# A dense PEER stage: one of four token blocks sums its down projection in two PSUM banks over all 128 chunks, the other blocks' sums take turns in four

## The chip, the cores and the metric

The kernel runs on one core of a Trainium2 chip. The metric is device time in microseconds, from the first to the last instruction with what lies around them. TensorE (PE) multiplies, VectorE (DVE) and ScalarE (ACT) do elementwise work, GpSimd (POOL) here mostly issues gathers, SyncE (SP) issues loads. PE writes only to PSUM, which has 8 banks of 128 partitions x 512 float32; DVE and ACT read it from there.

## What is computed

One decoder layer on 1024 tokens of 1024 floats: a token mixer (attention and a recurrence), and then PEER, a retrieval over 16,384 experts of one neuron each. The change touches only the last part:

```python
def blk(args):
    x_b, idx_b, g_b = args            # 128 tokens, 128 expert indices each, gates
    u = u_tab[idx_b]
    h = jax.nn.gelu(jnp.einsum('td,ted->te', x_b, u), approximate=False) * g_b
    return jnp.einsum('te,ted->td', h, v_tab[idx_b])
...
ffn = _peer_ffn(x, peer_w_q[l], peer_sub_keys[l], peer_u[l], peer_v[l])
x = _layer_norm(DEEPNORM_ALPHA * x + ffn, ln_ffn_g[l], ln_ffn_b[l])
```

`u_tab` and `v_tab` are 16,384 x 1024 float32.

## The kernel before

The eight blocks of 128 tokens are treated in two ways. Blocks 0, 1, 6 and 7 (`GATHER`) fetch the chosen rows of both tables by indirect DMA: per block 128 gathers of u rows (`gather_u`, L1105 on POOL), each reduced against the tokens by one DVE instruction (L1124), and then 128 gathers of v rows, each added into `ys` by one DVE instruction (L1149; the first by L1147, and `finish`, L1228, ends the block; block 0 does this on PE into the PSUM tile `y` instead). Eight tiles `rows` hold the rows under way.

Blocks 2 to 5 (`DENSE`, 512 tokens) compute all 16,384 experts as dense matmuls, with a matrix of gates that is zero where an expert was not chosen. The experts go in 128 chunks of 128, four chunks to a group (`JG`), 32 groups (`NG`). For each chunk, `up` loads 128 rows of u, splits them into a high and a low part (`uh` on ACT at L1031, `ul` on DVE at L1032), multiplies them with the tokens into a bank `psh` (8 slices, three matmuls each in `mm3`: L293, L294, L295), takes gelu (ACT, L1045), multiplies with the gates (DVE, L1047, `hs`), and splits again (`hh` on ACT, L1048, `hl` on DVE, L1049). `down` then works on a group in two halves `n` of 512 columns. For each chunk it loads and splits half the rows of v (`vh`, `vl`), and adds three matmuls for each of the four token blocks into that block's bank. After the four chunks of a half, DVE adds the four banks into `dy` in SBUF (L1064), which starts as the scaled residual. `finish_dense` normalises `dy` and writes it out.

PSUM's eight banks are pools: two `psh`, three `psf`, one `psv` (`BANKS`), and two for the tile `y` of `gather_v`. A half of `down` takes three `psf` and the `psv`.

The loop over groups takes two steps of `down` of the group before (a step is one chunk of one half), one chunk of `up`, and then `tick("dense")`, which lets the gathers of u and v rows of the other blocks emit 5.4 rows each a tick, while there are jobs. A scheduler then sets the order of each engine's instructions by its own estimates, so the order on an engine is fixed ahead of the run, and every engine works it off in order. The instructions on gathered rows keep their program order among each other.

Of the kernel before, what the change touches and what calls it, by code (L numbers as in the profile page):

```python
# [8 lines left out]
F32 = mybir.dt.float32  # L9
# [9 lines left out]
D = 1024  # L19
S = 1024  # L20
P = 128
# [45 lines left out]
ND = len(DENSE)  # L67
TD = ND * P
GS = float(2 ** 14)
JG = 4  # L70


class Layer:
# [249 lines left out]
    def mixers(self, groups, es):  # L323
# [6 lines left out]
        for n, (t0, T) in enumerate(groups):  # L330
# [48 lines left out]
            if T == 256:  # L379
                tail = self.tail_gather(t0, T, tail)  # L380
                if late:
                    return dense, tail, tl
                self.drain([tail])
                self.hold = HOLD
            else:
                self.tailed = False
                self.bjobs.append(self.tail_gbuild(tail, tl, gb))
# [631 lines left out]
    def dense(self, prep, tail, tl):  # L1019
        y, xh, xl = prep  # L1020
        nc, a = self.nc, self.a
        NG = P // JG
        dws = ExitStack()
        with self.pool("dw", 2, "left") as dw, dws:
            dv = {}
            def split(dw, src, n, name, bufs, raws):
                hi = dw.tile([P, n], F32R, name=name + "h", tag=name + "h", bufs=bufs)
                lo = dw.tile([P, n], F32R, name=name + "l", tag=name + "l", bufs=bufs)
                raw = dw.tile([P, n], F32, name=name + "r", tag=name + "r", bufs=raws)
                nc.sync.dma_start(raw, src)  # L1030
                nc.scalar.activation(hi, raw, AF.Copy)  # L1031
                nc.vector.tensor_tensor(lo, raw, hi.bitcast(F32), op=ALU.subtract)  # L1032
                return hi, lo

            def up(g):
                gt = dw.tile([P, TD // 32, JG, 32], F32, name="gt", tag="gt")
                nc.sync.dma_start(gt, self.d_g[:, :, g * JG : (g + 1) * JG, :].rearrange("q j i t -> j q i t"))
                for c in range(JG):
                    hh, hl = (dw.tile([P, TD], F32R, name=n, tag=n, bufs=JG + 2) for n in ("hh", "hl"))
                    uh, ul = (t.rearrange("p (c j) -> p c j", c=DC) for t in split(dw, a["ut"][g * JG + c], D, "u", 2, 3))  # L1040
                    ps = self.bank("h")[:, :TD]
                    for dc in range(DC):
                        self.mm3(ps, uh[:, dc], ul[:, dc], xh[:, dc], xl[:, dc], dc == 0, dc == DC - 1)
                    hs = dw.tile([P, TD], F32, name="hs", tag="hs")
                    nc.scalar.activation(hs, ps, AF.Gelu)  # L1045
                    h3 = hs.rearrange("p (q t) -> p q t", t=32)
                    nc.vector.tensor_tensor(h3, h3, gt[:, :, c], op=ALU.mult)  # L1047
                    nc.scalar.activation(hh, hs, AF.Copy)  # L1048
                    nc.vector.tensor_tensor(hl, hs, hh.bitcast(F32), op=ALU.subtract)  # L1049
                    yield hh, hl  # L1050

            def down(g, hs):
                for n in range(2):
                    ns = slice(n * 512, (n + 1) * 512)
                    acc = [self.bank("f") for _ in range(ND - 1)] + [self.bank("v")]
                    for c in range(JG):
                        r0 = (g * JG + c) * P
                        vh, vl = split(dv[0], a["v"][r0 : r0 + P, ns], 512, "v", 2, VRAW)
                        for tb in range(ND):
                            ts = slice(tb * P, (tb + 1) * P)  # L1060
                            self.mm3(acc[tb], hs[c][0][:, ts], hs[c][1][:, ts], vh, vl, c == 0, c == JG - 1)
                        yield
                    for tb in range(ND):
                        nc.vector.tensor_tensor(y[:, tb, ns], y[:, tb, ns], acc[tb], op=ALU.add)  # L1064
                        if g == NG - 1:
                            self.ln_stats(dv[1], tb, y[:, tb], (n,))

            def late():
                yield from tail
                tl.close()  # L1070
                dv[0] = dws.enter_context(self.pool("dv", 2, "left"))
                self.lnf = self.ffn_rows([dv[0].tile([P, D], F32, name=n, tag=n, bufs=1) for n in ("dlg", "dlb")])

            late, c0 = late(), 0
            prev = iter(())
            for g in range(NG + 1):
                cur = up(g) if g < NG else iter(())
                live, h = True, []
                while live:
                    live = False  # L1080
                    for _ in range(2):
                        if next(prev, self) is not self:
                            live = True
                    r = next(cur, self)
                    if r is not self:
                        live = True
                        h.append(r)
                    if live:
                        self.tick("dense", None, W0 if g == 0 else 1.0)
                    if c0 != 2:  # L1090
                        next(late, None)
                    c0 += 1
                self.drain([late])
                if g == NG - 1:
                    dv[1] = dv[0].tile([P, ND, 2, 6], F32, name="lnst", tag="lnst", bufs=1)
                if h:
                    prev = down(g, h)
            self.finish_dense(dv[0], y, dv[1])
# [218 lines left out]
```

## Time and profile before

| | |
|---|---|
| Median of 3 runs | 3072.04 us (3071.37 to 3078.85) |
| The profiled execution | 3059.49 us, of which 3057.6 from the first to the last instruction |
| Busy: PE, DVE, ACT, POOL | 85%, 87%, 36%, 53% |
| Mean granted TensorE clock | 0.921 of full |
| HBM traffic | 289 GB/s over the span |

"Busy" is the share of the span in which an engine ran something. PE's matmuls are pipelined, and one's end overlaps the next one's start, so for PE the distance from start to start says more than busy time. The same holds, less so, for DVE.

### The profile page before, as it was taken

To read this page: it belongs to the slowest core of one execution; us is meant where nothing else is said; L and a number is where in the kernel's file an instruction comes from. 1 tells how busy PE (TensorE), PEld (TensorE's weight loads), DVE (VectorE), ACT (ScalarE), POOL (GpSimd) and SP (SyncE) were. 2 spreads that over 40 slices of the span, in tenths; PEclk is the share of its full clock that TensorE was granted. 3 is DMA by queue.
4 is the path that set the end of the run, shared out by engine and by line. 5 is a ranking of instruction groups with operands and counts; after the bars stand their busy time and mean duration, and the time that the engine had idled before them with its cause. 6 is when DMAs were issued, how large, how long until landed. Compare 5 with 4: busy or idle time off the path is not lost.

```text
span 3057.6 us, 45196 instructions
## 1 busy us (share of the span) xinstructions
PE 2614.2 (85%) x15865; PEld 2140.4 (70%) x15865; DVE 2667.8 (87%) x5555; ACT 1091.4 (36%) x2068; POOL 1612.5 (53%) x1216
## 2 busy tenths in 40 slices
PE   7778699877669768779578999899989999999995
PEld 6768589755567545568457878777768877877874
DVE  8658776588778998689898999899999999999998
ACT  4733222365312233677522323232223323223321
POOL 2344377655665645110156666565476665656652
PEclk9878899878889879889789999999999999999998
DMA  7632499855877867865589999999999999999994
GB/s 278 195 138 90 178 333 326 256 157 163 303 279 270 288 199 255 312 258 194 192 305 343 361 366 381 333 370 368 345 355 363 372 386 362 359 361 342 371 334 164
DMA packets 338660, 887.11 MB, mean 290 GB/s; under 512 B 29912, under 2 KB 124136, under 8 KB 336000
## 3 DMA queue, kind: packets, MB, share of 16 engines
q0 software_dynamic: 147456, 536.94, 48.3%
q1 hardware_dynamic: 185200, 338.38, 31.7%
q10 hardware_dynamic: 5776, 8.90, 0.8%
q8 instruction: 125, 2.05, 0.3%
q14 instruction: 103, 0.84, 0.1%
HBM read 821.67 MB, written 62.42 MB: 289 GB/s over the span
## 4 chain that ended last, share of the span: by engine, by line
PE 40%; DVE 37%; issue 9%; DMA 6%; ACT 4%; POOL 3%; SPq 0%; DVEq 0%; POOLq 0%; ACTq 0%
DVE ys L1149 7%; PE psf L294 6%; PE psf L295 6%; PE psf L293 5%; DVE rows L1124 5%; PE psh L293 5%; PE psh L295 5%; PE psh L294 5%; POOL rows L1105 2%; DMA rows<-in_u,gsel 1%; DVE tw L808 1%; DVE dy L1064 1%; PE psv L294 1%; PE psv L718 1%; PE psv L295 1%
## 5 line engine op out<-in xcount | busy, mean ns | idle before, releaser
L1105 POOL DMA_INDIRECT rows<-in_u,gsel x512 | 688.4, 1345 | 585.6 <-DVE rows L1124 368.8
L1105 POOL DMA_INDIRECT rows<-in_v,gsel x512 | 640.9, 1252 | 437.7 <-DVE ys L1149 271.2
L1124 DVE SCALAR_TENSOR_TENSOR rows<-rows,gx 128x1024 f32<-128x1024 f32 x512 | 635.6, 1291 | 36.6 <-DMA rows<-in_u,gsel 27.8
L1149 DVE SCALAR_TENSOR_TENSOR ys<-rows,sd,ys 128x1024 f32<-128x1024 f32 x381 | 491.2, 1289 | 0.6
L293 PE MATMUL psh<-dxh,uh 128*128 128x512 f32 x1024 | 403.0, 394 | 29.4 <-ACT uh L1031 16.6
L295 PE MATMUL psh<-dxh,ul 128*128 128x512 f32 x1024 | 401.1, 392 | 9.5 <-DVE ul L1032 9.4
L294 PE MATMUL psh<-dxl,uh 128*128 128x512 f32 x1024 | 400.6, 391 | 0.0
L294 PE MATMUL psf<-vl,hh 128*128 128x512 f32 x768 | 311.0, 405 | 42.2 <-DVE vl L1032 41.4
L1031 ACT ACTIVATE vh<-vr 128x512 fp32r<-128x512 f32 x256 | 161.8, 632 | 436.1 <-PE psv L295 396.1
L295 PE MATMUL psf<-vh,hl 128*128 128x512 f32 x768 | 306.4, 399 | 0.0
L293 PE MATMUL psf<-vh,hh 128*128 128x512 f32 x768 | 278.5, 395 | 10.7 <-DVE dy L1064 8.8
L1031 ACT ACTIVATE uh<-ur 128x1024 fp32r<-128x1024 f32 x128 | 135.8, 1062 | 405.1 <-PE psh L294 400.0
L293 PEld LDWEIGHTS psh<-dxh,uh 128*128 128x128 f32 x1024 | 193.6, 189 | 77.2 <-ACT hs L1045 20.4
L295 PEld LDWEIGHTS psh<-dxh,ul 128*128 128x128 f32 x1024 | 193.5, 189 | 50.4 <-DVE ul L1032 10.5
L294 PEld LDWEIGHTS psh<-dxl,uh 128*128 128x128 f32 x1024 | 193.5, 189 | 39.5
L294 PEld LDWEIGHTS psf<-vl,hh 128*128 128x128 f32 x768 | 148.1, 193 | 89.7 <-DVE vl L1032 59.0
L215 ACT ACTIVATE whi<-wraw 128x1024 fp32r<-128x1024 f32 x106 | 111.6, 1056 | 230.9 <-PE psf L294 64.8
L1032 DVE TENSOR_TENSOR vl<-vr,vh 128x512 fp32r<-128x512 f32 x256 | 170.7, 689 | 12.0 <-ACT vh L1031 11.9
L293 PEld LDWEIGHTS psf<-vh,hh 128*128 128x128 f32 x768 | 145.5, 190 | 48.1 <-DVE dy L1064 9.8
L218 DVE TENSOR_TENSOR wlo<-wraw,whi 128x1024 fp32r<-128x1024 f32 x60 | 81.8, 1365 | 100.8 <-ACT whi L215 98.0
L295 PEld LDWEIGHTS psf<-vh,hl 128*128 128x128 f32 x768 | 148.1, 193 | 29.8
L1032 DVE TENSOR_TENSOR ul<-ur,uh 128x1024 fp32r<-128x1024 f32 x128 | 156.6, 1224 | 11.5 <-ACT uh L1031 10.5
(342 smaller groups left out, 6156.5 us busy)
## 6 DMA issues: line engine op xcount, KB each, us to landing
ur<-in_ut SPq DMA_DIRECT2D x128, 512.0 KB
vr<-in_v SPq DMA_DIRECT2D x256, 256.0 KB
d_g<-slab SPq DMA_DIRECT2D x16, 2048.0 KB
gt<-d_g SPq DMA_DIRECT2D x32, 1024.0 KB
wraw<-in_wq SPq DMA_DIRECT2D x48, 512.0 KB
wraw<-in_wt SPq DMA_DIRECT2D x34, 512.0 KB
wraw<-in_wn SPq DMA_DIRECT2D x24, 512.0 KB
wraw<-in_wo SPq DMA_DIRECT2D x24, 512.0 KB
```

Source lines behind the costliest of these rows:

```text
L215: nc.scalar.activation(hi, raw, AF.Copy)
L218: eng.tensor_tensor(lo, raw, hi.bitcast(F32), op=ALU.subtract)
L293: mm(out, lh, rh, start=start, stop=False, **kw)
L294: mm(out, lh, rl, start=False, stop=False, **kw)
L295: mm(out, ll, rh, start=False, stop=stop, **kw)
L718: nc.tensor.matmul(pv[:, qb], ps[:, qb * P : (qb + 1) * P], V[:, kb], start=kb == 0, stop=kb == b0 + qb, skip_group_check=True)
L808: nc.vector.match_replace(w, out_v[:, 0:8], vals, FMIN)
L1031: nc.scalar.activation(hi, raw, AF.Copy)
L1032: nc.vector.tensor_tensor(lo, raw, hi.bitcast(F32), op=ALU.subtract)
L1105: self.nc.gpsimd.indirect_dma_start(out=t, out_offset=None, in_=tab, in_offset=bass.IndirectOffsetOnAxis(ap=idx, axis=0))
L1124: self.pin(nc.vector.scalar_tensor_tensor(u, u, 1.0, x2, op0=ALU.mult, op1=ALU.mult, accum_out=sd[:, n : n + 1]), "u")
L1149: self.pin(nc.vector.scalar_tensor_tensor(ys, v, h, ys, op0=ALU.mult, op1=ALU.add), "w")
```

## The change

Block 0 of the dense blocks (`tb == 0`) gets the two-bank PSUM tile `y`, one bank for each half, and keeps adding into it from the first chunk to the last: its first matmul of all starts the sum, its last ends it. Its banks are added into `dy` only in the last group. The other three blocks still start anew in every group and half, and are added to `dy` each time. Their six sums in a group take `psf`, `psf`, `psf` in the first half and `psv`, `psf`, `psf` in the second.

```diff
--- before.py
+++ after.py
@@ -1049,18 +1049,24 @@
                     nc.vector.tensor_tensor(hl, hs, hh.bitcast(F32), op=ALU.subtract)
                     yield hh, hl
 
+            whole = [None]
+
             def down(g, hs):
+                if g == 0:
+                    whole[0] = self.psy.tile([P, D], F32, name="y", tag="y")
                 for n in range(2):
                     ns = slice(n * 512, (n + 1) * 512)
-                    acc = [self.bank("f") for _ in range(ND - 1)] + [self.bank("v")]
+                    acc = [whole[0][:, ns]] + [self.bank("v" if n and tb == 1 else "f") for tb in range(1, ND)]
                     for c in range(JG):
                         r0 = (g * JG + c) * P
                         vh, vl = split(dv[0], a["v"][r0 : r0 + P, ns], 512, "v", 2, VRAW)
                         for tb in range(ND):
                             ts = slice(tb * P, (tb + 1) * P)
-                            self.mm3(acc[tb], hs[c][0][:, ts], hs[c][1][:, ts], vh, vl, c == 0, c == JG - 1)
+                            first, last = (g == 0, g == NG - 1) if tb == 0 else (True, True)
+                            self.mm3(acc[tb], hs[c][0][:, ts], hs[c][1][:, ts], vh, vl, first and c == 0,
+                                     last and c == JG - 1, skip_group_check=tb == 0)
                         yield
-                    for tb in range(ND):
+                    for tb in range(0 if g == NG - 1 else 1, ND):
                         nc.vector.tensor_tensor(y[:, tb, ns], y[:, tb, ns], acc[tb], op=ALU.add)
                         if g == NG - 1:
                             self.ln_stats(dv[1], tb, y[:, tb], (n,))
```

After the change lines behind `down` have numbers 6 higher (the adds are L1070, v rows L1155).

The order of instructions moves in the dense stage alone. On DVE, beside v rows, the end of a half, before: the four adds into `dy` (L1064) alternate with v rows (L1149).

```order
L1149 SCALAR_TENSOR_TENSOR ys<-rows,sd,ys 128x1024
L1064 TENSOR_TENSOR dy<-dy,psf 128x512
L1149 SCALAR_TENSOR_TENSOR ys<-rows,sd,ys 128x1024
L1064 TENSOR_TENSOR dy<-dy,psf 128x512
L1149 SCALAR_TENSOR_TENSOR ys<-rows,sd,ys 128x1024
L1064 TENSOR_TENSOR dy<-dy,psf 128x512
L1149 SCALAR_TENSOR_TENSOR ys<-rows,sd,ys 128x1024
L1064 TENSOR_TENSOR dy<-dy,psv 128x512
L1047 TENSOR_TENSOR hs<-hs,gt 128x512
```

The end of a half at a like place after the change (L1070 are the adds, L1155 the v rows):

```order
L1155 SCALAR_TENSOR_TENSOR ys<-rows,sd,ys 128x1024
L1070 TENSOR_TENSOR dy<-dy,psf 128x512
L1155 SCALAR_TENSOR_TENSOR ys<-rows,sd,ys 128x1024
L1070 TENSOR_TENSOR dy<-dy,psf 128x512
L1155 SCALAR_TENSOR_TENSOR ys<-rows,sd,ys 128x1024
L1070 TENSOR_TENSOR dy<-dy,psf 128x512
L1155 SCALAR_TENSOR_TENSOR ys<-rows,sd,ys 128x1024
L1047 TENSOR_TENSOR hs<-hs,gt 128x512
```

Three adds stand there instead of four; the v rows are as many.

On PE, the start of the second half of group 13, before: the up pass (`psh`) ends, then come the first matmuls of the half (L293, `vh`), one for each block, with two matmuls of the next chunk's up pass among them, and then the first that need `vl` (L294).

```order
L295 MATMUL psh<-dxh,ul 128x512
L293 MATMUL psf<-vh,hh 128x512 x3
L293 MATMUL psh<-dxh,uh 128x512
L294 MATMUL psh<-dxl,uh 128x512
L293 MATMUL psv<-vh,hh 128x512
L294 MATMUL psf<-vl,hh 128x512
L295 MATMUL psf<-vh,hl 128x512
```

The same place after the change, where `y` is block 0's bank:

```order
L295 MATMUL psh<-dxh,ul 128x512
L293 MATMUL y<-vh,hh 128x512
L294 MATMUL y<-vl,hh 128x512
L295 MATMUL y<-vh,hl 128x512
L293 MATMUL psv<-vh,hh 128x512
L294 MATMUL psv<-vl,hh 128x512
L295 MATMUL psv<-vh,hl 128x512
L293 MATMUL psf<-vh,hh 128x512
```

Each block's three matmuls now stand together, block 0's first, and nothing of the up pass stands among them; the first use of `vl` comes one matmul after the first use of `vh` instead of six.

## Rows read from the trace of the kernel before

**Rows 1.** The page: the span, busy time of each engine, and the busy tenths of PE and DVE in 40 equal slices of the span.

```profile
span 3057.6 us, 45196 instructions
...
PE 2614.2 (85%) x15865; PEld 2140.4 (70%) x15865; DVE 2667.8 (87%) x5555; ACT 1091.4 (36%) x2068; POOL 1612.5 (53%) x1216
...
PE   7778699877669768779578999899989999999995
...
DVE  8658776588778998689898999899999999999998
```

**Rows 2.** Busy time by stretch: us from the span's start, length, busy us (and instructions) of PE, PE's weight loads, DVE, ACT and POOL, the granted clock, the share of the DMA engines, and GB/s. Two stretches beside gathered u rows, three beside v rows, and the dense stage as a whole.

```profile
1830.00:1918.00 88.00, 87.83 (x386) 71.67 (x385) 81.70 (x133) 27.24 (x41) 56.97 (x42) 1.00 1.00 370
2305.00:2438.00 133.00, 132.64 (x579) 107.81 (x579) 130.45 (x213) 41.22 (x61) 90.71 (x65) 1.00 1.00 370
1980.00:2207.00 227.00, 220.47 (x960) 179.00 (x959) 224.54 (x248) 67.66 (x101) 132.79 (x106) 1.00 0.97 359
2535.00:2718.00 183.00, 177.15 (x771) 143.82 (x770) 180.93 (x200) 55.18 (x81) 107.05 (x88) 1.00 0.99 362
2769.00:2905.00 136.00, 132.69 (x579) 108.51 (x580) 134.73 (x151) 41.25 (x61) 91.92 (x66) 1.00 0.97 357
1560.00:3037.00 1477.00, 1405.47 (x6022) 1136.02 (x6020) 1427.36 (x1924) 428.40 (x632) 910.45 (x679) 0.98 0.96 353
```

**Rows 3.** Groups of instructions between 1560 and 3037 us: line, engine, operation, out<-in, shapes, count, then busy us and mean ns of one, then idle us before them and what ended most of it.

```profile
L1149 DVE SCALAR_TENSOR_TENSOR ys<-rows,sd,ys 128x1024 f32<-128x1024 f32 x381 | 491.2, 1289 | 0.6
...
L1032 DVE TENSOR_TENSOR vl<-vr,vh 128x512 fp32r<-128x512 f32 x256 | 170.7, 689 | 12.0 <-ACT vh L1031 11.9
...
L1032 DVE TENSOR_TENSOR ul<-ur,uh 128x1024 fp32r<-128x1024 f32 x122 | 149.4, 1225 | 4.4 <-ACT uh L1031 3.4
...
L1064 DVE TENSOR_TENSOR dy<-dy,psf 128x512 f32<-128x512 f32 x192 | 126.4, 681 | 1.6 <-PE psf L295 1.6
...
L1047 DVE TENSOR_TENSOR hs<-hs,gt 128x512 f32<-128x512 f32 x124 | 85.6, 691 | 2.1 <-ACT hs L1045 1.3
...
L1064 DVE TENSOR_TENSOR dy<-dy,psv 128x512 f32<-128x512 f32 x63 | 43.0, 682 | 0.0
```

**Rows 4.** Instructions of PE in order of time within an up pass: start us, us. Nineteen matmuls lie between these two.

```profile
2507.16 0.39 PE L293 MATMUL psh<-dxh,uh 128*128 128x512 f32 x1
...
2511.70 0.39 PE L295 MATMUL psh<-dxh,ul 128*128 128x512 f32 x1
```

**Rows 5.** Instructions of DVE in order of time, beside u rows (L1124) and then beside v rows (L1149): start us, us.

```profile
1904.71 1.22 DVE L1124 SCALAR_TENSOR_TENSOR rows<-rows,gx 128x1024 f32<-128x1024 f32 x1
...
1905.85 1.22 DVE L1124 SCALAR_TENSOR_TENSOR rows<-rows,gx 128x1024 f32<-128x1024 f32 x1
...
1907.00 1.88 DVE L1064 TENSOR_TENSOR dy<-dy,psf 128x512 f32<-128x512 f32 x3
...
2492.37 0.69 DVE L1064 TENSOR_TENSOR dy<-dy,psv 128x512 f32<-128x512 f32 x1
2492.97 1.28 DVE L1149 SCALAR_TENSOR_TENSOR ys<-rows,sd,ys 128x1024 f32<-128x1024 f32 x1
2494.16 0.69 DVE L1032 TENSOR_TENSOR vl<-vr,vh 128x512 fp32r<-128x512 f32 x1
2494.76 1.28 DVE L1149 SCALAR_TENSOR_TENSOR ys<-rows,sd,ys 128x1024 f32<-128x1024 f32 x1
...
2505.13 1.22 DVE L1032 TENSOR_TENSOR ul<-ur,uh 128x1024 fp32r<-128x1024 f32 x1
2506.26 1.28 DVE L1149 SCALAR_TENSOR_TENSOR ys<-rows,sd,ys 128x1024 f32<-128x1024 f32 x1
2507.46 0.68 DVE L1064 TENSOR_TENSOR dy<-dy,psf 128x512 f32<-128x512 f32 x1
```

**Rows 6.** Who waited for whom between 1560 and 3037 us: us in total, times, the longest.

```profile
POOL rows L1105 <- DVE ys L1149: 284.3, 287, 11.5
...
PE psf L294 <- DVE vl L1032: 41.4, 25, 7.6
...
PE psf L293 <- DVE dy L1064: 8.8, 5, 3.1
...
DVE ys L1147 <- DMA rows<-in_v,gsel: 6.8, 1, 6.8
...
PE psv L293 <- DVE dy L1064: 5.4, 3, 2.7
```

**Rows 7.** The switch between u and v rows: where the v blocks begin (L1147) and end (L1228) with the first and last start, and then DVE's and PE's instructions at the first switch, with the idle time before them and what ended it.

```profile
L1147 DVE TENSOR_SCALAR ys<-rows,sd x3: 743/744/755, 1919.2 to 2748.0; 128x1024 f32<-128x1024 f32 x3
...
L1228 DVE SCALAR_TENSOR_TENSOR rows<-rows,ys x3: 1217/1220/1220, 2204.8 to 3020.1; 128x1024 f32<-128x1024 f32 x3
...
1919.22 0.76 DVE L1147 TENSOR_SCALAR ys<-rows,sd 128x1024 f32<-128x1024 f32 x1 [6.80 <-DMA rows<-in_v,gsel]
...
1928.11 0.79 PE L294 MATMUL psf<-vl,hh 128*128 128x512 f32 x1 [6.33 <-DVE vl L1032]
```

**Rows 8.** Busy time in one piece of 10 us, columns as in Rows 2.

```profile
1990.00:2000.00 10.00, 10.00 (x45) 8.27 (x45) 9.96 (x12) 3.33 (x5) 8.48 (x6) 1.00 1.04 408
```

**Rows 9.** The last instructions of block 0's gather that read the PSUM tile `y` (ACT): count, ns min/median/max, first and last start.

```profile
L1199 ACT ACTIVATE rows<-y x12: 371/374/378, 1308.2 to 1313.6; 32x256 f32<-32x256 f32 x12
```

## The prediction, made before the changed kernel was run

> **What bounds the kernel now.** I read the page first. In its 40 slices both PE and DVE stand at 8 and 9 from the 22nd to the last but one [rows 1]: that is the dense stage, about 1550 to 3037 us, the only stage the change touches. Two engines that are both nearly full are told apart only inside a stretch, so I cut the stage into stretches that hold nothing but groups of four chunks, and counted PE's matmuls in each [rows 2]. A group has 192 matmuls: 4 chunks x 8 slices x 3 in the up pass, and 2 halves x 4 chunks x 4 blocks x 3 in the down pass. So a group lasts 192 x 88 / 386 = 43.8 us and 192 x 133 / 579 = 44.1 us in the two stretches where the gather beside it is of u rows, and 45.4, 45.6 and 45.1 us in the three where it is of v rows (the v blocks begin at L1147 and end at L1228 [rows 7]).
>
> Next, what each engine needs for one group. PE: 21 matmuls start within 4.54 us, 0.227 us apart [rows 4], so 192 take 43.6 us. DVE: its instructions overlap a little, so I take distances between starts, not durations [rows 5]: 0.60 us for each of the 512-wide ones (vl, hs, hl and the adds into dy), 1.13 for ul, 1.195 for a v row, 1.145 for a u row (1904.71 to 1907.00 is two). A group has 8 vl, 4 ul, 4 hs, 4 hl and 8 adds: 4.8 + 4.5 + 4.8 + 4.8 = 18.9 us. Gathered rows per group I counted in the order of DVE's instructions: the three v blocks (384 rows) stand beside 24, 23 and 22 chunks, 17.25 groups, so 22.3 rows or 26.6 us; the u rows (308) beside 57 chunks, 14.25 groups, 21.6 rows or 24.7 us. Sums:
>
> - v group: DVE 45.5 us, PE 43.6, measured 45.4. **DVE bounds it**, with PE 1.8 us short of work.
> - u group: DVE 43.6, PE 43.6, measured 44.0. **Both bound it**, and the balance costs about 0.4 us.
>
> The waits say the same: PE waited 41.4 us in all for vl from DVE, and 8.8 and 5.4 us for a bank that an add had not yet emptied [rows 6]. POOL waited 284 us for v rows' buffers that DVE had not yet read. These five stretches are 767 of the window's 1477 us and lose 24 us against PE's 0.227; the other 710 us hold 6022 - 3275 = 2747 matmuls, 624 us, and so lose some 86 (less by the records that are missing). That goes mostly at the switches from u to v and back: at the first of them DVE stood 6.8 us before the first v row for its transfer, and PE 6.3 us behind it for vl [rows 7].
>
> **The change part by part.** *Adds removed:* before, 32 groups x 2 halves x 4 blocks = 256 adds ([rows 3]: 192 with psf, and 63 of the 64 with psv within the window). After, block 0 is added only in the last group: 194. 62 fewer, at 0.60 us, are 37 us of DVE, 1.2 us a group. Nothing hides DVE in a v group, so there it counts until PE becomes the later one.
>
> - v group: DVE 45.5 - 1.2 = 44.3, PE 43.6. The nearest row for two engines so close is the u stretch, 0.4 us over when equal; with 0.7 us between them I take 0.2. So 44.5 instead of 45.4: 0.9 us x 17.25 = **15.5 us**. Bounds: nothing, and PE's own 43.6, 1.8 x 17.25 = 31 us.
> - u group: DVE 42.4, PE 43.6 stays. Only the cost of the balance can go: I take 0.3 of 0.4 us, x 14.25 = **4.3 us**. Bounds 0 and 6.
>
> *Banks:* eight sums took turns in four banks: a half took all four, so the next half's first matmuls came in one by one as adds emptied them. The order of PE shows it before (three psf, two of the up pass, then psv) and not after. The six sums left use three of four banks a half, and block 0 never waits. What this can give is the 8.8 + 5.4 = 14.2 us that PE waited for adds. Nearly all of it lies at the switches, where DVE works off a backlog, and there the next thing PE needs, vl, is late from the same engine. I take **3 us**; bounds 0 and 14.
>
> *Costs that I put at nothing.* The matmuls are as many and as wide as before. The two y banks were last read at about 1314 us [rows 9], 270 us before the first add of the dense stage, so the first matmul does not wait for them. The last group adds all four blocks, so the tail after the last matmul is unchanged. ACT has no instruction more or less. Loads are the same; POOL's order is identical in both, and its gathers wait for DVE, so they follow DVE's gain.
>
> Sum: 15.5 + 4.3 + 3 = **23 us**. The profiled execution took 3059.5 us (span 3057.6 and 1.9 around it) and would take about 3036; the median shown is 12.5 us above that execution, and from it the same 23 us give 3049.
>
> *A rule that speaks against it.* The dense stage moves 357 to 370 GB/s [rows 2], so DMA could be what paces it. The rows answer: the stretches with u move 370 GB/s for 88 and 133 us, single 10 us pieces reach 408 [rows 8], and within v blocks DVE waited for a transfer only at the first row of one [rows 3, 6]. A v group of 44.5 us needs 361 x 45.4 / 44.5 = 368 GB/s, what the u stretches have. The Trainium skill (DMA: Bandwidth & Descriptors, "Where 436 GB/s comes from") says that for transfers between HBM and SBUF the HBM side binds, at about 358 GB/s a core; by that sentence alone the v groups would already be at the limit and nothing would be gained. This trace is above that figure for whole stretches, so it binds here no more than the first rival below.
>
> **The rivals.**
>
> 1. *DMA paces the v groups after all.* For it: DMA's share is 0.97 to 1.00, and v stretches stay at 357 to 362. Against it: the 370 above. Price: no gain but what the u groups may give, 3068 to 3072.
> 2. *The relief goes into later vl.* After the change PE's order is tighter: the orders of PE shown with the change have a half's start where vl is needed by the 7th matmul before and by the 2nd after. Counted over all 256 half chunks, the matmuls from a half chunk's first to its first use of vl fall from 6.55 to 4.35 on average, 2.2 x 0.227 = 0.5 us less cushion. If a fifth of that (25 us of 128) turns into waits, the gain is eaten: 3072 or so.
> 3. *Slower, by the same cushion.* From a quarter of it on (32 us) the kernel is more than 0.3% slower; if all of it is lost in the v groups' 138 half chunks, 69 - 23 = 46 us slower, 3118. Against it: PE waited for vl 25 times in 256, 41 us in all, a good part of it at the switches, and what makes vl late there is DVE's load, which falls.
> 4. *More than forecast:* v groups come down to PE's 43.6 us, the u balance and all bank waits go: 31 + 6 + 14 = 51 us, 3021.
> 5. *The change doesn't do what it says* would need block 0's matmuls to wait on something else; PE's order shows them at the head of each half with only vh and hh behind them. I give it nothing.
>
> **How the numbers follow.** About 0.3% (9 us) is what a measurement of this kernel can tell from no change. Forecast, 9 to 37 us gained (37 is all of the saved DVE time): 0.70. Rival 4, 37 to 51 us: 0.08. Rival 1: 0.08. Rival 2: 0.07. Rival 3: 0.07. So faster 0.78, same 0.15, slower 0.07. The predicted time is 3049 us. The range 3028 to 3070 takes the forecast, half of rival 4, and half of rivals 1 and 2, whose times lie within 9 us around 3072; it leaves out their other half and rival 3.
>
> **What the profile after would show.** 194 adds instead of 256 and some 37 us less DVE time. Groups beside v rows at about 44.5 us (over 195 matmuls in 45.4 us), with PE above 98% there instead of 97; groups beside u rows at 43.7. PE's waits for adds near nothing, its wait for vl not above 41 us. DMA at about 368 GB/s in the v stretches. If v groups stay at 45.4 with DVE idle for transfers, rival 1 was right; if DVE is idle for PE and PE for vl, rivals 2 or 3. The 86 us outside the stretches should be nearly as they are; if they shrink by more than the 3 us, the forecast is too small.

## The result and the profile after

The changed kernel takes 3053.1 us (median of 7) where the kernel before took 3078.9 us (median of 7) beside it: a ratio of 0.9925, 95% interval 0.9906 to 0.9944, or some 26 us less. Run again it took 3035.0 us against 3056.5: 0.9926 [0.9911, 0.9941], 22 us less. The forecast was faster, by 23 us, to 3049. Each ratio below is to runs of the kernel before on the same chip.

The work ahead of the dense stage, which the change leaves as it was, took between 1499 and 1529 us up to the first dense gelu (L1045) in the profiled runs of this study, which were made on several chips, so stages are compared here, not spans. From the first dense gelu to the end, two profiles of the kernel before have 1543.3 and 1543.4 us, and two of the changed kernel 1525.1 and 1528.3.

The page after, answering to [rows 1], and the chain that ended last by engine:

```profile
span 3054.1 us, 45032 instructions
...
PE 2609.3 (85%) x15865; PEld 2142.4 (70%) x15865; DVE 2624.6 (86%) x5493; ACT 1093.1 (36%) x2068; POOL 1637.3 (54%) x1216
...
PE   7777699878679768779569899999979999999995
...
DVE  8658767588768987679988899999989999999998
...
PE 53%; DVE 29%; issue 7%; DMA 6%; ACT 3%; POOL 2%; another core or an unknown queue 0%; SPq 0%; DVEq 0%; POOLq 0%; ACTq 0%
```

DVE has 62 instructions and 43 us less, and PE stands for 53% of the chain and DVE for 29%, where the page before has 40 and 37%. PE's row has a single 7 among the nines of the dense stage, in the 30th slice; that place has a part of its own below.

Busy time by stretch, columns and order as in [rows 2]: two stretches beside u rows, three beside v rows, the dense stage.

```profile
1806.00:1938.00 132.00, 132.00 (x579) 107.74 (x578) 128.28 (x208) 41.23 (x61) 94.68 (x65) 1.00 1.02 377
2317.00:2449.00 132.00, 132.00 (x577) 107.36 (x576) 129.40 (x210) 41.03 (x61) 92.12 (x66) 1.00 1.00 372
1989.00:2209.00 220.00, 218.80 (x965) 180.53 (x964) 218.62 (x239) 68.77 (x101) 143.00 (x103) 1.00 0.98 365
2502.00:2721.00 219.00, 217.70 (x957) 179.30 (x957) 218.18 (x240) 67.84 (x101) 147.96 (x107) 1.00 1.01 380
2820.00:2952.00 132.00, 131.13 (x576) 107.71 (x576) 131.41 (x143) 40.84 (x61) 80.00 (x66) 1.00 1.01 379
1560.00:3037.00 1477.00, 1405.55 (x6071) 1145.34 (x6071) 1408.07 (x1891) 431.90 (x635) 947.87 (x681) 0.98 0.97 356
```

Counted as the prediction did, 192 matmuls beside v rows take 192 x 220 / 965 = 43.8 us, 43.9 and 44.0; before it was 45.4, 45.6 and 45.1. PE is busy 99.3 to 99.5% of these stretches instead of 97. Beside u rows it is 43.8 and 43.9.

Who waited for whom, 1560 to 3037 us, answering to [rows 6]:

```profile
POOL rows L1111 <- DVE ys L1155: 213.2, 242, 6.8
...
PE y L294 <- DVE vl L1032: 41.4, 14, 17.6
PE psf L293 <- DVE dy L1070: 17.9, 5, 6.0
...
PE psh L293 <- ACT hs L1045: 2.7, 4, 1.0
```

The instructions that write `dy` (count; shortest, median and longest in ns; first and last start) show the 194 adds: 160 + 32 + 2. The two with `y` are the last group's.

```profile
L1070 DVE TENSOR_TENSOR dy<-dy,psf x160: 667/678/690, 1601.7 to 3033.8; 128x512 f32<-128x512 f32 x160
L1070 DVE TENSOR_TENSOR dy<-dy,psv x32: 667/680/689, 1624.0 to 3031.4; 128x512 f32<-128x512 f32 x32
...
L1070 DVE TENSOR_TENSOR dy<-dy,y x2: 680/684/687, 3006.4 to 3030.7; 128x512 f32<-128x512 f32 x2
```

To see where the time went I cut the changed kernel's dense stage at the start of every fourth gelu: group 0 begins at the first. The kernel before is cut at the same counts of PE's matmuls, since its own gelus don't always stand behind the same work: between the gelus that bound groups 15 and 16 it has 360 matmuls, the changed kernel 384, and those 24 are 5.4 us. Mean of two profiles each, us; PE's floor is 0.2267 us a matmul, 43.52 a group of 192 (0.227 by [rows 4]; the last digit is from the fastest stretch below, 960 matmuls in 217.60 us).

| groups | beside them | matmuls | before | after | change | floor |
|---|---|---|---|---|---|---|
| 0–6 | start, u rows | 1268 | 334.0 | 332.8 | -1.2 | 287.4 |
| 7–9 | u gives way to v | 576 | 143.5 | 138.8 | -4.7 | 130.6 |
| 10–14 | v rows | 960 | 227.5 | 219.3 | -8.1 | 217.6 |
| 15, 16 | v gives way to u | 384 | 102.9 | 109.0 | **+6.1** | 87.0 |
| 17–19 | u rows | 576 | 132.4 | 131.8 | -0.6 | 130.6 |
| 20–25 | u to v, then v rows | 1152 | 275.4 | 272.1 | -3.3 | 261.1 |
| 26, 27 | one v block to the next | 384 | 97.5 | 100.4 | +2.9 | 87.0 |
| 28–30 | v rows | 576 | 138.9 | 132.0 | -6.9 | 130.6 |
| 31, end | | | 93.7 | 92.9 | -0.8 | |

The sum is 16.6 us. Two profiles of one program agree within 0.1 us in groups 10 to 14 and within 0.5 in 15 to 25 and 28 to 30, so there this cut sees tenths of a microsecond where spans and medians see several. In groups 0 to 9 they differ by up to 2.2 us, in 26 and 27 by up to 3.5, so the changes of rows 0–6 and 26, 27 can't be told from none. Groups 10 to 14 serve as the gauge for all experiments. The window of the kernel before, and then of the changed one:

```profile
1991.21:2218.67 227.46, 220.93 (x962) 179.37 (x961) 225.08 (x263) 68.22 (x101) 130.50 (x106) 1.00 0.98 361
```

```profile
2000.57:2219.89 219.32, 218.12 (x962) 179.97 (x961) 217.00 (x252) 68.20 (x101) 144.04 (x106) 1.00 0.98 365
```

PE issues 962 matmuls in both. DVE issues 11 instructions fewer, ten adds and a `ul` that now falls just outside, and the window is 8.1 us shorter. PE's waits in it were these before:

```profile
PE psf L294 <- DVE vl L1032: 3.8, 6, 1.0
PE psh L293 <- ACT hs L1045: 2.7, 4, 0.7
```

After the change one wait of 1.2 us for `vl` is left.

### The profile page after: what moved, and what is told of

The parts are those of the page before. It is cut to its first block, busy times and chain, and to the rows that moved or that the text cites. A ratio compares the mean times of both kernels' runs of the same rounds, so it can differ in the third digit from the quotient of the medians.

```text
span 3054.1 us, 45032 instructions
## 1 busy us (share of the span) xinstructions
PE 2609.3 (85%) x15865; PEld 2142.4 (70%) x15865; DVE 2624.6 (86%) x5493; ACT 1093.1 (36%) x2068; POOL 1637.3 (54%) x1216
## 4 chain that ended last, share of the span: by engine, by line
PE 53%; DVE 29%; issue 7%; DMA 6%; ACT 3%; POOL 2%; another core or an unknown queue 0%; SPq 0%; DVEq 0%; POOLq 0%; ACTq 0%
PE psf L295 7%; PE psf L294 7%; PE psf L293 6%; PE psh L295 6%; PE psh L293 6%; PE psh L294 6%; DVE rows L1130 4%; DVE ys L1155 3%; PE y L294 2%; PE y L295 2%; PE y L293 1%; DVE tw L808 1%; POOL rows L1111 1%; PE psv L718 1%; PE psf L681 1%
## 5 line engine op out<-in xcount | busy, mean ns | idle before, releaser
L1111 POOL DMA_INDIRECT rows<-in_v,gsel x512 | 660.1, 1289 | 397.5 <-DVE ys L1155 213.2
L1155 DVE SCALAR_TENSOR_TENSOR ys<-rows,sd,ys 128x1024 f32<-128x1024 f32 x381 | 488.8, 1283 | 4.1 <-DMA rows<-in_v,gsel 3.4
L293 PE MATMUL psh<-dxh,uh 128*128 128x512 f32 x1024 | 400.9, 392 | 19.5 <-ACT uh L1031 16.4
L294 PE MATMUL psh<-dxl,uh 128*128 128x512 f32 x1024 | 400.1, 391 | 0.0
L293 PE MATMUL psf<-vh,hh 128*128 128x512 f32 x640 | 239.5, 396 | 18.0 <-DVE dy L1070 17.9
L294 PE MATMUL psf<-vl,hh 128*128 128x512 f32 x640 | 253.2, 396 | 0.0
L295 PE MATMUL psf<-vh,hl 128*128 128x512 f32 x640 | 252.7, 395 | 0.0
L293 PEld LDWEIGHTS psh<-dxh,uh 128*128 128x128 f32 x1024 | 193.4, 189 | 62.0 <-ACT uh L1031 16.7
L295 PEld LDWEIGHTS psh<-dxh,ul 128*128 128x128 f32 x1024 | 193.4, 189 | 50.7 <-DVE ul L1032 10.5
L294 PEld LDWEIGHTS psh<-dxl,uh 128*128 128x128 f32 x1024 | 193.2, 189 | 40.0
L293 PEld LDWEIGHTS psf<-vh,hh 128*128 128x128 f32 x640 | 121.2, 189 | 49.2 <-DVE dy L1070 24.0
L218 POOL TENSOR_TENSOR wlo<-wraw,whi 128x1024 fp32r<-128x1024 f32 x46 | 112.5, 2449 | 67.9 <-ACT whi L215 63.8
L294 PE MATMUL y<-vl,hh 128*128 128x512 f32 x256 | 105.5, 412 | 41.6 <-DVE vl L1032 41.4
```

The lines of the kernel that those rows point to most:

```text
L218: eng.tensor_tensor(lo, raw, hi.bitcast(F32), op=ALU.subtract)
L293: mm(out, lh, rh, start=start, stop=False, **kw)
L294: mm(out, lh, rl, start=False, stop=False, **kw)
L295: mm(out, ll, rh, start=False, stop=stop, **kw)
L1111: self.nc.gpsimd.indirect_dma_start(out=t, out_offset=None, in_=tab, in_offset=bass.IndirectOffsetOnAxis(ap=idx, axis=0))
L1155: self.pin(nc.vector.scalar_tensor_tensor(ys, v, h, ys, op0=ALU.mult, op1=ALU.add), "w")
```

## The place that gave 6 us back

In groups 15 and 16 the changed kernel is slower than the kernel before. The stretch between the gelus that bound them, before and then after, columns as in [rows 2]: 11.7 us longer, of which 24 matmuls more are 5.4.

```profile
2218.67:2315.89 97.22, 86.71 (x362) 69.06 (x361) 92.99 (x151) 26.85 (x41) 67.77 (x48) 0.96 0.96 355
```

```profile
2219.89:2328.77 108.88, 90.71 (x386) 72.94 (x384) 97.37 (x155) 28.55 (x42) 67.38 (x48) 0.92 0.96 346
```

DVE's instructions there, after the change (start us, us; most rows left out):

```profile
2209.18 0.64 DVE L1032 TENSOR_TENSOR vl<-vr,vh 128x512 fp32r<-128x512 f32 x1
...
2212.26 0.15 DVE L234 TENSOR_TENSOR rst<-rsy 128x1 f32<-128x1 f32 x1
2212.33 1.22 DVE L1130 SCALAR_TENSOR_TENSOR rows<-rows,gx 128x1024 f32<-128x1024 f32 x1
...
2226.72 1.23 DVE L1130 SCALAR_TENSOR_TENSOR rows<-rows,gx 128x1024 f32<-128x1024 f32 x1 [0.23 <-DMA rows<-in_u,gsel]
...
2229.61 0.68 DVE L1049 TENSOR_TENSOR hl<-hs,hh 128x512 fp32r<-128x512 f32 x1
2230.21 3.36 DVE L1130 SCALAR_TENSOR_TENSOR rows<-rows,gx 128x1024 f32<-128x1024 f32 x1
...
2238.09 1.28 DVE L1032 TENSOR_TENSOR vl<-vr,vh 128x512 fp32r<-128x512 f32 x2
```

Between one `vl` and the next lie 29 us. The v block has just ended, and the small operations of its layernorm (L231 to L257, each waiting for the one before) stand in DVE's order with u rows between them, ten in all; five more rows follow. PE, meanwhile:

```profile
2238.82 0.79 PE L294 MATMUL y<-vl,hh 128*128 128x512 f32 x1 [17.56 <-DVE vl L1032]
2239.41 0.63 PE L295 MATMUL y<-vh,hl 128*128 128x512 f32 x1
...
2243.25 0.43 PE L295 MATMUL y<-vh,hl 128*128 128x512 f32 x1
```

The same place in pieces of 10 us, columns as in [rows 2]:

```profile
2220.00:2230.00 10.00, 1.21 (x5) 0.34 (x3) 8.18 (x17) 2.34 (x3) 3.62 (x5) 0.81 1.04 390
2230.00:2240.00 10.00, 1.19 (x3) 0.99 (x4) 10.00 (x14) 0.00 (x0) 8.93 (x5) 0.50 0.90 302
2240.00:2250.00 10.00, 10.00 (x39) 8.07 (x38) 5.08 (x7) 1.26 (x2) 5.00 (x5) 0.83 0.95 371
```

PE stood 17.6 us for this one `vl`, and its granted clock fell to 0.50, the level of 1.2 GHz: the matmuls after the wait start 0.427 us apart until 2243.25, then 0.227 again, some 2 us more. In the kernel before, DVE's order has the same ten rows and the same five, but a `vl` between them:

```profile
2223.65 1.23 DVE L1124 SCALAR_TENSOR_TENSOR rows<-rows,gx 128x1024 f32<-128x1024 f32 x1
...
2226.54 0.69 DVE L1032 TENSOR_TENSOR vl<-vr,vh 128x512 fp32r<-128x512 f32 x1
2227.14 2.89 DVE L1049 TENSOR_TENSOR hl<-hs,hh 128x512 fp32r<-128x512 f32 x1
2229.95 1.21 DVE L1124 SCALAR_TENSOR_TENSOR rows<-rows,gx 128x1024 f32<-128x1024 f32 x1
```

There PE's longest wait in these two groups was 5.9 us. Of the 11.7 us between the two waits the two groups lost 6.1 by the table, since before the change PE also stood for other things there. So the total of PE's waits for `vl`, 41.4 us on both sides, hides two opposite moves: in groups 10 to 14 they nearly vanished (before six waits, now one; in the whole window 25 and 14), and 18 us of what remains is one wait.

## The experiments

The theory: DVE bounds the v groups, so what counts is the DVE time of the 62 adds. The main rival: what counts is that the next half need not wait for banks, or PE's order that follows from it. Four kernels take the two apart.

**The banks without the saving.**

```diff
-first, last = (g == 0, g == NG - 1) if tb == 0 else (True, True)
+first, last = True, True
-for tb in range(0 if g == NG - 1 else 1, ND):
+for tb in range(ND):
```

> The changed kernel's banks (block 0 in the two y banks, six sums in four), but block 0 starts anew in every group and is added to dy after every half as before: 256 adds, the DVE work of the kernel before. Theory (the 62 adds that are saved are DVE time, and DVE bounds the groups beside v rows): nearly nothing is gained, 0 to 6 us against the kernel before, v groups at 45 to 45.5 us. Rival (the gain is the bank that the next half need not wait for): most of the 26 us is there, 18 us or more, v groups at 43.6 to 44.

Measured: 1.0024 [1.0009, 1.0038] of the kernel before. Groups 10 to 14:

```profile
1976.16:2203.62 227.46, 220.91 (x962) 179.30 (x961) 225.07 (x263) 68.25 (x102) 131.44 (x106) 1.00 0.98 362
```

To the hundredth what the kernel before has. The banks without the saving are worth nothing here; nor did they take the waits away, PE waited 14.3 us for adds between 1560 and 3037 us, where [rows 6] has 14.2. The 0.24% more, where 0 to 6 us less was expected, lie mostly in groups 15 and 16, 110.4 us instead of 102.9 for the same 384 matmuls; of that no cause was isolated.

**The saving without the banks.**

```diff
-acc = [whole[0][:, ns]] + [self.bank("v" if n and tb == 1 else "f") for tb in range(1, ND)]
+acc = [whole[0][:, ns]] + [self.bank("f") for tb in range(1, ND)]
```

> Block 0 is summed in the y banks over all 128 chunks (194 adds), but the three other sums of a half always take the same three banks, so a half can start blocks 1 to 3 only behind the adds of the half before, as in the kernel before; the psv bank lies idle. Theory (DVE time): 18 to 26 us less than before, v groups at 43.6 to 44.2. Rival (banks): 0 to 6 us less, v groups at 45 or more, and PE's wait for adds into dy at 14 us or above.

Measured: 0.9923 [0.9904, 0.9941], the whole gain. Groups 10 to 14:

```profile
1974.20:2193.51 219.31, 218.11 (x962) 179.97 (x961) 217.25 (x252) 68.19 (x102) 143.23 (x106) 1.00 0.98 366
```

PE's wait for adds between 1560 and 2990 us:

```profile
PE psf L293 <- DVE dy L1070: 17.3, 7, 6.0
```

That is more than the 14.2 us of [rows 6], and the kernel is as fast as the changed one. The wait for banks is not a term of the sum. This kernel, too, has the wait of 17.5 us for one `vl` in groups 15 and 16.

**The changed kernel with as many adds put back**, into a tile that nothing reads:

```diff
+if g < NG - 1:
+    jk = dw.tile([P, 512], F32, name="jk", tag="jk", bufs=1)
+    nc.vector.tensor_tensor(jk, y[:, 0, ns], y[:, 1, ns], op=ALU.add)
```

> The changed kernel with one 512-wide DVE add per half into a tile that nothing reads (62 in all, both operands in SBUF), in the place of the adds that the change takes away. It frees no bank and delays none. Theory (DVE time): the gain is given back, 0 to 6 us less than before, v groups at 45 or more. Rival (the gain is in banks or in the order of PE): 20 us or more of the gain stay, v groups under 44.

Measured: 1.0024 [1.0013, 1.0035]. The gain is gone with the DVE time put back: the kernel is some 7 us slower than before, a little past the 0 to 6 us less that were expected. Groups 10 to 14 take 230.0 us, with DVE busy 224.25 in them. That is 2.5 us more than in the kernel before, which has as many adds; this order leaves DVE idle for 5.7 us there instead of 2.4, and why was not looked into.

**Half the saving.** Block 0's sum runs over two groups, 224 adds:

```diff
-first, last = (g == 0, g == NG - 1) if tb == 0 else (True, True)
+first, last = (g % 2 == 0, g % 2 == 1) if tb == 0 else (True, True)
-for tb in range(0 if g == NG - 1 else 1, ND):
+for tb in range(g % 2 == 0, ND):
```

> The changed kernel, with block 0 summed over two groups at a time: 224 adds, half of the saving (18 us of DVE time). Theory (DVE time, as far as PE's floor lets it count): about half the gain, 9 to 16 us less than before, v groups about 44.7 us. Rival (what counts is that the next half finds block 0's bank free, or the order of PE): the whole gain, 20 us or more, or nothing, under 5.

Measured beside the second run of the changed kernel: 0.9958 [0.9942, 0.9974], 13 us less than before, against 22. Groups 10 to 14: 224.9 us with 965 matmuls instead of 960, or 44.8 us for 192 of them, about halfway between 45.5 and 43.9.

> The changed kernel once more, beside the three below. If its gain is what was measured first: 23 to 28 us less than the kernel before. Its profile is a second one of the same program: if the work ahead of the dense stage varies from run to run, the first dense gelu comes some 10 us earlier or later than the 1529 us of the first profile, with the dense stage within 4 us of its 1525.

The first gelu came at 1506.2 us, 23 us earlier than in the first profile, the dense stage took 1528.3 us, and the gain was 22 us, a little below what was expected.

**The other direction:** the three lines of padding put into the kernel before, 62 adds more than it had.

> The kernel before with one more 512-wide DVE add per half into a tile that nothing reads: 62 more, 37 us of DVE time, 1.2 us a group, the change's step in the other direction. Theory (DVE bounds v groups and is level with PE in u groups): v groups 1.2 us longer and u groups 0.9 to 1.2, 17.25 x 1.2 + 14.25 x 1.0 = 35 us slower, 25 to 42. Rival (DVE has slack that such work fits in, and the gain came from somewhere else): under 15 us slower.

Measured: 1.0164 [1.0151, 1.0178], 50 us slower, the theory's way but more than the 42 it allowed.

```profile
1992.83:2226.17 233.34, 223.06 (x962) 180.27 (x961) 231.95 (x279) 69.56 (x102) 130.33 (x105) 0.99 0.97 351
```

Groups 10 to 14 went as worked out: 5.9 us more for ten adds, 0.59 us each, the distance between starts of [rows 5] and not the 0.68 us that one lasts. DVE is busy 99.4% there. Groups 17 to 19 (u) took 0.7 us more each. The surplus is mostly in groups 15 and 16 (+9.4 us, of which 2 would be the adds) and 20 to 27 (+18.0, of which 10 would be): again where one kind of row gives way to another. Why it is more there than the adds was not isolated.

**Further in the same direction.** Blocks 0 and 1 both summed to the end (block 1 in two `psf` banks, so that blocks 2 and 3 have one `psf` and `psv` for every half):

```diff
+two[:] = [self.bank("f"), self.bank("f")]        # at g == 0
-acc = [whole[0][:, ns]] + [self.bank("v" if n and tb == 1 else "f") for tb in range(1, ND)]
+acc = [whole[0][:, ns], two[n], self.bank("f"), self.bank("v")]
-for tb in range(0 if g == NG - 1 else 1, ND):
+for tb in range(0 if g == NG - 1 else 2, ND):
```

and `tb < 2` where the change has `tb == 0`.

> Blocks 0 and 1 are both summed over all 128 chunks (block 1 in two psf banks held to the end), blocks 2 and 3 take the one psf bank and the psv bank that are left in every half: 132 adds, another 37 us of DVE time less than in the changed kernel. Theory (after the change PE bounds all groups, at 43.6 us): no more than the switches between u and v can give, 0 to 8 us less than the changed kernel. Rival (DVE still bounds v groups): another 15 to 25 us less. Third way (the two tight banks now hold PE back, since both sums left must wait for the adds of the half before): slower than the changed kernel, PE's wait for adds into dy above 40 us.

Measured: 0.9886 [0.9866, 0.9906], 35 us less than before, the best of all. Groups 10 to 14:

```profile
1977.89:2195.49 217.60, 217.60 (x962) 180.33 (x961) 214.87 (x247) 68.34 (x102) 133.82 (x104) 1.00 1.00 375
```

PE is busy every microsecond, 43.52 us a group, which single groups of the kernel before reach too, and DVE has 2.7 us to spare. The second 62 adds gained about 12 us by the ratios (0.9886 against 0.9925, each with 0.002 either way), somewhat above the 0 to 8 expected. In the profile the dense stage is 18 us shorter than the mean of the changed kernel's two (1508.7 against 1526.7): groups 10 to 14 gave 1.7 us, 28 to 30 1.5, and 20 to 25 3.1; most of the rest came from groups 7 to 9 (3.1), 15 and 16 (3.2) and 26 and 27 (4.4).

With a third block, in six banks, block 3 has to share the two `psh` banks with the up pass:

> Blocks 0, 1 and 2 are summed over all 128 chunks in six banks; block 3 takes turns with the up pass in the two psh banks: 70 adds, another 37 us of DVE time less than with two blocks. Theory (PE at 43.52 us a group is the floor now, and DVE's time counts at the switches between u and v alone): 0 to 8 us less than with two blocks, 35 to 46 us less than the kernel before; DVE's busy time falls by some 37 us with little to show for it. Rival (each 62 adds are worth another 12 us or more, as the second block was): 47 us or more less than before. Third way: block 3 and the up pass get in each other's way in two banks, slower than with two blocks, PE's waits for psh above 30 us.

Measured: 0.9907 [0.9887, 0.9926]: not faster than with two blocks, perhaps slower. Groups 10 to 14 take 217.60 us as with two, with DVE busy 3 us less. PE's waits from 1580 us on:

```profile
PE y L294 <- DVE vl L1032: 14.1, 6, 5.3
PE y L294 <- DVE lnve L254: 11.9, 1, 11.9
PE psh L293 <- DVE dy L1071: 9.5, 6, 7.1
```

Sharing the `psh` banks cost 9.5 us of waits for adds, under the 30 that the third way named. Against two blocks, groups 0 to 6 became 9.3 us longer, and 15, 16, 26 and 27 gave 10.5 us back. So in the clean groups beside gathered rows an add was worth about 0.6 us as long as DVE was the later engine, and nothing once PE was.

**The switch from v to u.** One line in the gather, at the end of a v block, lets the next u block start a chunk later:

```diff
             self.finish(ys, r0)
+            self.hold = 2
```

> The changed kernel with one line more: when a v block ends, the next u block starts one chunk later, so that its rows don't stand between the small operations of the v block's layernorm on DVE, ahead of the vl that PE wants. Theory (the 18 us wait for vl in the dense chunks 60 to 68, where v gives way to u, is an effect of DVE's order there, 11 and then 5 u rows ahead of vl; in the kernel before it was 5 rows fewer): that wait falls under 10 us and these eight chunks take 95 to 102 us instead of 109. What comes of it for the whole is open by up to 6 us, since some five u rows move towards the end: 12 us less to 3 us more than the changed kernel, 18 to 35 us less than before. Rival (the wait is the transfer of the first u rows, or PE's clock): the eight chunks stay at 107 to 111 us.

Measured: 0.9917 [0.9893, 0.9941]. In groups 15 and 16 PE's waits are now

```profile
PE psf L293 <- DVE dy L1070: 5.9, 1, 5.9
PE y L294 <- DVE vl L1032: 5.2, 1, 5.2
```

The wait of 17.6 us is 5.2, and the two groups take 103.2 us instead of 109.0, just outside the range expected. It is the order on DVE, then, that made this wait, and without it the two groups are back at the 102.9 us of the kernel before. The dense stage as a whole is 6 us shorter in the profile (1520.7 against 1525.1 and 1528.3), which the ratio's interval can't confirm. With two blocks the same line, together with 5.6 rows a chunk, gained nothing:

> Two blocks summed over all chunks, with the same line at the end of a v block and 5.6 instead of 5.4 gathered rows a chunk, which makes up for the rows that start later and uses DVE time that the second block freed. Theory (PE bounds the groups at 43.52 us and DVE has about 1 us a group to spare; 0.2 x 4 rows are 0.9 us): the groups stay at 43.5 to 43.8, and with the line at the switch 0 to 12 us less than two blocks alone, 35 to 48 us less than before. Rival (DVE is the bound again with more rows): groups beside v rows above 44.2 us and no gain over two blocks alone.

Measured: 0.9894 [0.9872, 0.9917]. The first v block stays at PE's floor, the second does not; five groups of 192 matmuls each:

```profile
1969.70:2187.52 217.82, 217.82 (x962) 179.95 (x961) 217.16 (x237) 67.82 (x100) 136.62 (x108) 1.00 1.02 386
2480.91:2702.56 221.65, 218.88 (x961) 179.84 (x960) 221.20 (x237) 67.51 (x100) 139.57 (x114) 1.00 1.03 388
```

These are 43.6 and 44.3 us a group, and in the second DVE is busy all but 0.5 us, so there the rival is right: with more rows DVE is the later engine again. The end after the last gelu falls from 58.0 to 43.9 us as the rows finish earlier, and this and the switches, which now fall in other groups, take it back: groups 10 to 27 last 833.1 us against 819.7, groups 7 to 9 142.2 against 135.7.

> A second profile of the kernel before. If the work ahead of the dense stage varies from run to run and the dense stage hardly: first dense gelu within 1500 to 1530 us, the dense stage 1543 us within 4, with the same groups long and short.

First gelu at 1527.4 us, dense stage 1543.4, the same groups long and short.

## Why the prediction came out, step by step

- **DVE bounds the v groups: right**, and shown from both sides: the adds alone carry the whole gain, the banks alone nothing, half the adds some half of it, and 62 more adds cost 1.2 us in each clean v group.
- **v groups at 44.5 us, 15.5 us gained: right in kind, too small.** They came to 43.8 to 44.0, and 43.86 in groups 10 to 14 (219.3 / 5), 1.63 us less each; by 17.25 that is 28 us, where I had 15.5. The step that failed is the sum for DVE, 45.5 us, which I let stand as DVE's pure need because it met the measured 45.4. It put all 384 v rows into 17.25 groups, 22.3 each; groups 10 to 14 hold 101 v and 6 u rows. With these the same sum is 101 x 1.195 + 6 x 1.145 + 5 x 18.9 = 222.1 us, 44.4 a group, where 45.5 were measured. So about 1 us a group was not in the sum: some 3 us in the five groups are small operations at the end of a v block, and DVE stood idle for 2.4 (227.46 - 225.08). Of the 8.1 us saved, ten adds at 0.60 and the `ul` at 1.13 make 7.1, and PE's waits fell from 6.5 us to 1.2. Done with the right count, the sum gives 44.4 - 1.2 = 43.2, or 43.8 with the small operations: level with PE's 43.52, not 0.7 us above it. PE's floor, not 44.5, was the thing to forecast from.
- **u groups 44.0 to 43.7: the right way, too much.** Groups 17 to 19 lost 0.2 us each. The groups at the start, which I had counted in, lost 1.2 us, less than the 2.2 by which two profiles differ there. So the 4.3 us are not shown; about 2 are seen.
- **Banks, 3 us: wrong.** PE's waits for adds went from 14.2 to 17.9 us rather than near nothing, and the kernel with tight banks is as fast. I took a wait in the trace for time that its removal gives back. Nor do the waits lie at the switches, as I wrote: 10.7 of the 14.2 us come behind the last gelu (2999.5 us), with the last group, where all four blocks are still added after the change. PE's waits for adds in the kernel before from 2999 us on:

```profile
PE psf L293 <- DVE dy L1064: 5.6, 2, 3.1
PE psv L293 <- DVE dy L1064: 5.1, 2, 2.7
```

- **The 86 us outside the clean stretches "nearly as they are": wrong in its parts.** Switches moved by -5 to +6 us. The worst, one wait for `vl`, is what rivals 2 and 3 described, but at one place and for another reason: not that a half needs its `vl` sooner, but that DVE's order puts 15 gathered rows ahead of it. Against the rivals as I put them: the matmuls between a half chunk's first and its first use of `vl` are 4.35 on average after the change, 2.6 with two blocks, and 8.8 with the banks alone; the fastest kernel has a smaller cushion than the changed one, and that with the largest is slower than before.
- **DMA paces it (rival 1): refuted.** The v stretches ran at 365 to 380 GB/s, and with two blocks at 375 for 217.6 us without a pause on PE. The sentence of the Trainium skill (DMA: Bandwidth & Descriptors, "Where 436 GB/s comes from") that the HBM side binds at about 358 GB/s does not hold for this core in these runs.
- **The total, 23 us.** That it is near the 22 and 26 measured is in part luck, because two errors cancel. I had some 12 us too little for the v groups. And where one kind of row gives way to another, which I had left as it was, about as much was given back: 28 us for the v groups and 2 for the u groups would be 30, and the stage is 16.6 us shorter in the profiles, 15.0 of it in the eight clean v groups. Groups 15 and 16 are 6.1 of what was given back; the rest was not taken apart. What isn't settled: the profiles' dense stages differ by 15 to 18 us, the medians by 22 and 26, each uncertain by about 5. The rest would have to lie ahead of the dense stage, where both programs have the same order and the profiled runs on one chip differ by up to 11 us.

## What to carry to other kernels

When two engines are level, removing work from one pays at its start-to-start distance until the other's floor, and no further: work out both floors. A sum that meets the measured time proves no bound by itself; count the instructions in the very stretch that was measured. Where a scheduler writes the order, look at the places where one kind of work gives way to another: one late operand there stopped PE for 17.6 us, and two groups became 6 us longer by a change that took work off DVE. And cut two programs at equal work before comparing their parts: the same cut at gelus would have shown 12 us for these 6.

## What the runs showed of the hardware

A stretch of the same instructions repeats to a hundredth: groups 10 to 14 took 227.46, 227.45 and 227.46 us in three profiles (two of the kernel before, one of the banks alone), and 217.60 twice at PE's floor, while the changed kernel's work ahead of the dense stage differed by 23 us between its two profiles. The padded kernel, with as many adds in another order, took 230.0 us, so the order counts too. And one core moved 375 GB/s for 217.6 us beside a PE that never paused.
